# A mixture-of-experts kernel whose experts' inputs are fetched by indirect DMA and transposed, instead of gathered by matmuls

## The chip, the cores and the metric

The kernel runs on one core of one Trainium2 chip. Its time is device microseconds from launch to end. The kernel before took 3032.44 us (median of three runs, 3029.88 to 3035.55). TensorE is called PE, VectorE DVE, ScalarE ACT, GpSimd POOL and SyncE SP, as in the profile.

## The reference, cut to what matters

The program is a chain of four layers: two first ones and two equal blocks, each of a mixing phase and a mixture of experts. The change is in the mixture. It takes 512 tokens of 1024 numbers, chooses for each token two of 16 experts (from the group of four that holds the best score), and sums the two experts' outputs with their weights:

```python
def grouped_moe(x2d, w_router, router_bias, w_gate, w_up, w_down):
    ...                                   # scores, best group, two experts per token, weights
    buf_tok = jnp.full((P,), T, jnp.int32).at[dest].set(tok_flat[order])
    ...
    xb = x_pad[buf_tok].reshape(n_blocks, EXPERT_BLOCK, D)
    def expert_block(args):
        xblk, e = args
        h = jax.nn.silu(xblk @ w_gate[e]) * (xblk @ w_up[e])
        return h @ w_down[e]
    yb = lax.map(expert_block, (xb, blk_expert))
    y = yb.reshape(P, D) * buf_gate[:, None]
    return jax.ops.segment_sum(y, buf_tok, num_segments=T + 1)[:T]
```

All tensors are float32. The three weight matrices of one expert are 1024 x 512, 1024 x 512 and 512 x 1024, 6.3 MB together, so that the 16 experts of a layer read 100.7 MB.

## The kernel before, in words

Every float32 product is made of three matmuls of numbers that are split into a high and a low part (`mm3` and `tm`, lines L184 to L186): high by high, low by high, high by low. A weight chunk of 512 KB comes from memory on SP's queue (`wload`, L1602) into one of nine raw buffers (five named `mr`, four named `wr`); ACT casts it to the high part (`wsplit`, L1616), DVE subtracts to get the low part (L1617). A raw buffer is free for the next chunk when that subtraction has read it. Ten chunks are asked for before the experts begin.

Each expert owns 128 slots. Tokens beyond that go to overflow blocks, which a loop with a run-time count works through before the experts (`For_i` in `moe`). For an ordinary pair of experts `expert_slots` (L1650) compares each token's rank with the slot numbers, eight comparisons of 128 x 128, which give a 0/1 matrix `oh` for two experts. These run on DVE for experts 0 and 1 and on POOL for all others. `expert_in` multiplies the normed tokens, kept in SBUF as a high and a low part (`xs`, tiles named `x`), by that matrix: 64 matmuls of 128 x 256 at L1639, whose results are the pair's inputs, already transposed (`xg`, high part `xgh`, low part `xgl`). So the gather and the transposition are one product. `expert_up` multiplies by the gate and up weights, 48 matmuls, multiplies the two (`hs`, L1661 on DVE), and transposes `hs` by four matmuls at L1664; `expert_down` multiplies by the down weights, 24 matmuls, and writes the rows to a table `yd` in memory through ACT's queue. Experts are pipelined by one: expert e's up product is followed by the down product of expert e-1.

After expert 14's rows are written, eight indirect DMAs on POOL's queue (L1751) fetch, for each of four tiles of 128 tokens, the rows of its two experts out of `yd` into tiles `yg`; `add` (L1760, DVE) and `combine` (PE and DVE, L1768 to L1771) sum them with the token's own normed input. Expert 15's output does not go through `yd`; the matrix `oh` of its slots, transposed, spreads it over the tokens.

The order on each engine is made by a scheduler from its own estimates; `tc.issue_after(x)` holds instructions behind x. Buffers named `f4` (six of 128 x 1024) are shared by the matrices `oh`, the first gather of each token tile, and the raw weights of overflow blocks.

Of the kernel before, what the change touches and what calls it, by code (L numbers as in the profile page):

```python
# [18 lines left out]
P = 128  # L19
T = 512  # L20
# [28 lines left out]
class K:  # L49
# [1346 lines left out]
    def after_mix(self, l, xs, i0, gb, pl, sc, x1):  # L1396

        nc = self.nc
        tt = nc.vector.tensor_tensor
        st = self.ln_stats(xs[i0:i0 + 2])  # L1400
        u = self.small([2, 16], name="ru2")
        bc = lambda v: v[:, :, None].to_broadcast([P, 2, 16])
        bt = lambda v: v[:, None, :].to_broadcast([P, 2, 16])
        tt(u, bt(self.wsum[:, l, 0]), bc(st[:, 2]), op=OP.mult)
        tt(u, u, bt(self.wsum[:, l, 1]), op=OP.add)
        yield
        c = slice(i0, i0 + 2)
        tt(sc[:, c], pl[:, i0 * 16:(i0 + 2) * 16].rearrange("p (i e) -> p i e", i=2), bc(st[:, 1]), op=OP.mult)
        tt(sc[:, c], sc[:, c], u, op=OP.add)
        yield  # L1410
        late = i0 > 0
        for a in range(2):
            x = xs[i0 + a]
            t = self.x2()
            self.normal(x, st, a)
            for v in range(2):
                eng = AFFINE[late][a][v]
                with self.tc.issue_after(self.ranked.ins) if late else nullcontext():
                    getattr(nc, eng[0]).tensor_tensor(t[v], x[v], gb[0][v], op=OP.mult)  # L1419
                    getattr(nc, eng[1]).tensor_tensor(t[v], t[v], gb[1][v], op=OP.add)  # L1420
            h, lo = [self.wp.tile([P, D], F32R, name="x1", tag="xt", bufs=8) for _ in range(2)]
            x1[i0 + a] = h, lo
            for v in range(2):
                o = slice(v * 512, (v + 1) * 512)
                self.hi(h[:, o], t[v])
                with self.tc.issue_after(self.routed.ins) if late else nullcontext():
                    self.lo(lo[:, o], t[v], h[:, o])

    def moe_constants(self):
# [26 lines left out]
        for l in range(2):  # L1456
            for j, name in enumerate(("ln1_g_2", "ln1_b_2")):
# [7 lines left out]
                if j:  # L1465
                    nc.vector.tensor_tensor(s, s, rb, op=OP.add)
        self.yd = self.dp.tile([SLOTS, D], F32, name="yd")

    def clear_slots(self):

# [171 lines left out]
            xT += [(h[:, u * n:(u + 1) * n], lo[:, u * n:(u + 1) * n]) for u in range(2)]  # L1642
        return xT

    def expert_slots(self, rank, e, eng):

        oh = self.f4(F32R, "oh").rearrange("p (i a s) -> p i a s", i=4, a=2)
        for a in range(2):
            for i in range(4):
                eng.tensor_scalar(oh[:, i, a], self.iota, rank[:, i, e + a:e + a + 1], None, op0=OP.is_equal)  # L1650
        return oh.rearrange("p i a s -> p i (a s)")

    def expert_up(self, xT, wg, wu):

# [22 lines left out]
    def moe(self, l, xs, rt):  # L1677
# [10 lines left out]
        with tc.For_i(0, nov, 1) as b:  # L1688
# [9 lines left out]
            xT = self.expert_in(xs, oh.rearrange("p i a s -> p i (a s)"), 256)  # L1698
            hT = self.expert_up([[v[:, :P] for v in t] for t in xT], self.wrows(we[0], 8, True), self.wrows(we[1], 8, True))
            self.expert_down(hT, we[2], self.yd[bass.ds(row, P)], True)  # L1700
        oh = self.expert_slots(rank, 0, nc.vector)
        xT = self.expert_in(xs, oh, 256)
        hT = None
        f = []
        for e in range(16):
            if e % 2 == 0 and e < 14:
                oh = self.expert_slots(rank, e + 2, nc.gpsimd)
                nx = self.expert_in(xs, oh, 256)
            if e == 15:
                self.expert_down(hT, W[2][14], self.yd[14 * P:15 * P])  # L1710
            o = e % 2 * P
            h2 = self.expert_up([[v[:, o:o + P] for v in t] for t in xT],
                                *[self.wrows(W[j][e], 8, first=first.pop(0) if first else None) for j in range(2)])
            if e == 2:
                slot, wv, wl = self.weigh(oh1, oh2, sc, slotf)
            if e == 13:
                after = self.last_pe
            if e == 14:
                for i in range(4):
                    with tc.issue_after(after.ins):  # L1720
                        f.append(self.x2())
                        for h in range(2):
                            o = slice(h * 512, (h + 1) * 512)
                            nc.gpsimd.tensor_tensor(f[i][h], xs[i][0][:, o].bitcast(F32), xs[i][1][:, o].bitcast(F32), op=OP.add)
            if 0 < e < 15:
                self.expert_down(hT, W[2][e - 1], self.yd[(e - 1) * P:e * P])
            hT = h2
            if e % 2:
                xT = nx

        pt = self.pt()
        for i in range(4):
            nc.tensor.transpose(pt[:, i * P:(i + 1) * P], oh[:, i, P:].bitcast(F32), self.ident)
        ct = self.t2(F32R, "ct")
        nc.scalar.copy(ct, pt)
        pw = self.pt()
        for i in range(4):
            nc.tensor.matmul(pw[:, :1], oh[:, i, P:].bitcast(F32), wl[:, i:i + 1], start=i == 0, stop=i == 3)
        dg = self.t2(F32, "dg")
        for i in range(2):  # L1740
            for j in range(2):
# [29 lines left out]
                nc.vector.tensor_tensor(f[i][h], f[i][h], ps, op=OP.add)  # L1771

        y = []
        for c in range(2):
            py = self.pj()
            ws2 = list(self.wsplit(raws[c]))
            if c:
                for i in range(2):
                    for j in range(2):
                        add(i, j)  # L1780
            for k, wk in enumerate(ws2):
                self.mm3(py, hT[k], wk, k == 0, k == 3)
                if c == 1 and k == 1:
# [183 lines left out]
```

## Time and profile before

| | |
|---|---|
| median of three runs | 3032.44 us |
| profiled execution: its own time, span | 3038.98 us, 3037.2 us |
| busy PE, DVE, ACT, POOL | 2896.9, 1951.3, 1557.7, 271.0 us |
| DMA moved, mean rate | 453.48 MB, 149 GB/s |
| matmuls at L1639 | 1088, 136.2 us busy |
| granted TensorE clock, mean | 0.981 |

Busy shares are means over a span whose stages differ. Slice 22 of the 40 begins near 1595 us and holds the start of the first block's experts; the second block's experts fill slices 36 to 40. The DMA share of a window is the mean busy share of 16 DMA engines; a share near 1.00 reads as all of them busy, and the sum of packet times can come a little over it.

### The profile page before, as it was taken

The page shows a single profiled execution, that of the slowest core. Times are in us where ns is not written, and L with a number is a line of the kernel's source. Part 1 is how long each engine was busy: PE and PEld are TensorE (multiplying, and loading weights), DVE is VectorE, ACT ScalarE, POOL GpSimd, SP SyncE. Part 2 cuts the span into 40 slices and gives each one's busy share as a digit, 9 for nine tenths or more (in the row PEclk, how much of TensorE's full clock was granted, in tenths as well). Part 3 has the DMA queues.
Part 4 walks back from the last instruction along what each step waited for, and adds up shares of the span by engine and source line. Part 5 has one row for each costly group of instructions (what it writes and reads, how often), then busy time and mean ns, then how long its engine had stood idle before and what let it go on. Part 6 is the DMA issues. An engine that isn't in the chain of part 4 may idle for free. (4 is left out here: it accounts for less than half of the span.)

```text
span 3037.2 us, 44080 instructions
## 1 busy us (share of the span) xinstructions
PE 2896.9 (95%) x16635; PEld 2454.0 (81%) x16635; DVE 1951.3 (64%) x3817; ACT 1557.7 (51%) x2717; POOL 271.0 (9%) x282
## 2 busy tenths in 40 slices
PE   8999999999999999999989999879999999699996
PEld 6888878876669998878888888669987878588874
DVE  4454467576656776444477878978744345777788
ACT  4343377466655455223345777535542244476774
POOL 0000000000000000000027000440000000260023
PEclk9999999999999999999999999989999999899998
DMA  4242325431026222322365988931223335378996
GB/s 133 85 148 81 105 84 160 141 91 36 25 84 205 70 60 66 97 88 80 103 201 196 330 320 322 320 98 59 64 78 96 90 111 167 112 277 302 326 324 239
DMA packets 335599, 453.48 MB, mean 149 GB/s; under 512 B 24374, under 2 KB 208408, under 8 KB 335384
## 3 DMA queue, kind: packets, MB, share of 16 engines
q1 hardware_dynamic: 320856, 421.78, 42.1%
q10 hardware_dynamic: 12224, 20.46, 1.8%
q0 software_dynamic: 2304, 8.39, 0.8%
q8 instruction: 132, 2.16, 0.3%
q14 instruction: 83, 0.68, 0.1%
HBM read 421.69 MB, written 28.88 MB: 148 GB/s over the span
## 5 line engine op out<-in xcount | busy, mean ns | idle before, releaser
L164 DVE TENSOR_TENSOR wl<-wr,wh 128x1024 fp32r<-128x1024 f32 x348 | 422.9, 1217 | 441.1 <-ACT wh L163 436.9
L163 ACT CAST wh<-wr 128x1024 fp32r<-128x1024 f32 x352 | 363.1, 1033 | 579.9 <-PE pj L185 336.6
L184 PE MATMUL pj<-x,wh 128*128 128x512 f32 x1288 | 508.2, 395 | 0.6 <-ACT x L110 0.6
L185 PE MATMUL pj<-x,wh 128*128 128x512 f32 x1288 | 507.6, 394 | 0.0
L186 PE MATMUL pj<-x,wl 128*128 128x512 f32 x1288 | 506.3, 393 | 1.1 <-DVE wl L164 1.0
L186 PEld LDWEIGHTS pj<-x,wl 128*128 128x128 f32 x1288 | 241.9, 188 | 54.9 <-issue 4.7
L184 PEld LDWEIGHTS pj<-x,wh 128*128 128x128 f32 x1288 | 242.0, 188 | 52.6 <-issue 4.6
L185 PEld LDWEIGHTS pj<-x,wh 128*128 128x128 f32 x1288 | 242.0, 188 | 52.3 <-issue 5.6
L211 PE MATMUL pj<-wh,x 128*128 128x256 f32 x864 | 249.1, 288 | 3.8 <-DVE xb L277 3.1
L212 PE MATMUL pj<-wl,x 128*128 128x256 f32 x864 | 247.2, 286 | 0.0
L213 PE MATMUL pj<-wh,x 128*128 128x256 f32 x864 | 245.3, 284 | 0.0
L211 PE MATMUL pj<-wh,yh 128*128 128x256 f32 x640 | 181.6, 284 | 0.5 <-ACT wh L163 0.3
L212 PE MATMUL pj<-wl,yh 128*128 128x256 f32 x640 | 179.6, 281 | 1.5 <-DVE wl L164 1.5
L213 PE MATMUL pj<-wh,yl 128*128 128x256 f32 x640 | 179.1, 281 | 0.4 <-DVE yl L127 0.3
L211 PEld LDWEIGHTS pj<-wh,x 128*128 128x128 f32 x864 | 166.3, 193 | 5.2 <-DVE xb L277 3.5
L212 PEld LDWEIGHTS pj<-wl,x 128*128 128x128 f32 x864 | 166.6, 193 | 0.4
L213 PEld LDWEIGHTS pj<-wh,x 128*128 128x128 f32 x864 | 166.3, 193 | 0.3
L1639 PE MATMUL pt<-oh,x 128*128 128x256 f32 x1088 | 136.2, 287 | 18.4 <-DVE oh L1695 8.6
L1617 DVE TENSOR_TENSOR wl<-mr,wh 128x1024 fp32r<-128x1024 f32 x106 | 139.1, 1312 | 22.3 <-ACT wh L1616 22.2
L1639 PEld LDWEIGHTS pt<-oh,x 128*128 128x128 f32 x1088 | 135.3, 195 | 20.2 <-DVE oh L1695 8.7
L1617 DVE TENSOR_TENSOR ml<-mr,mh 128x1024 fp32r<-128x1024 f32 x108 | 135.9, 1258 | 21.5 <-ACT mh L1616 19.4
L1419 POOL TENSOR_TENSOR x<-x,bc 128x512 f32<-128x512 f32 x14 | 18.2, 1321 | 1255.7 <-ACT x L1328 1255.7
(503 smaller groups left out, 6607.0 us busy)
## 6 DMA issues: line engine op xcount, KB each, us to landing
wr<-in_w_in SPq DMA_DIRECT2D x124, 512.0 KB, 3.7
mr<-in_w_exp_gate SPq DMA_DIRECT2D x76, 512.0 KB, 6.6
mr<-in_w_exp_up SPq DMA_DIRECT2D x72, 512.0 KB, 5.5
mr<-in_w_exp_down SPq DMA_DIRECT2D x66, 512.0 KB, 5.9
wr<-in_w_exp_down SPq DMA_DIRECT2D x62, 512.0 KB, 6.3
wr<-in_hawk_w_in SPq DMA_DIRECT2D x60, 512.0 KB, 3.6
wr<-in_w_exp_up SPq DMA_DIRECT2D x56, 512.0 KB, 4.4
wr<-in_w_exp_gate SPq DMA_DIRECT2D x52, 512.0 KB, 6.9
```

Of the source, the lines that this page charges most:

```text
L163: self.nc.scalar.copy(wh[:, :kt, :c], raw[:, :kt, :c])
L164: eng.tensor_tensor(wl[:, :kt, :c], raw[:, :kt, :c], wh[:, :kt, :c].bitcast(F32), op=OP.subtract)
L184: mm(ps, a[0], b[0], start=first, stop=False)
L185: mm(ps, a[0], b[1], start=False, stop=False)
L186: mm(ps, a[1], b[0], start=False, stop=last)
L211: mm(d, tok(x[k][0]), w[k][0][:, :n], start=k == 0 and a == 0, stop=False, skip_group_check=True)
L212: mm(d, tok(x[k][0]), w[k][1][:, :n], start=False, stop=False, skip_group_check=True)
L213: mm(d, tok(x[k][1]), w[k][0][:, :n], start=False, stop=end, skip_group_check=True)
L1419: getattr(nc, eng[0]).tensor_tensor(t[v], x[v], gb[0][v], op=OP.mult)
L1617: self.nc.vector.tensor_tensor(wl, raw, wh.bitcast(F32), op=OP.subtract)
L1639: nc.tensor.matmul(pt[:, u * n:(u + 1) * n], xs[i][part][:, f], oh[:, i], start=i == 0 and part == 0, stop=i == 3 and part == 1)
```

## The change

The normed tokens are written to a table `x1d` in memory when they are made (`put`, eight stores of 256 KB per layer on SP's queue). `slot_tokens` works out on DVE, with eight small matmuls, which token sits in each slot of each expert (`idx`). `expert_fetch` then fetches the 128 rows of one expert by one indirect DMA on POOL's queue, 14 per layer, two experts ahead, and `expert_turn` transposes them by eight 128 x 128 matmuls and splits the result. Experts 0 and 1 and the overflow blocks keep the product with the 0/1 matrix; for expert 15 the matrix is still made, for the spread at the end. Seven of the eight pair products of a layer, 448 matmuls at L1639, and 52 of 56 comparisons on POOL are gone. The additions of token tiles 0 and 1 are held behind `mark`, the last split of expert 15's activations.

```diff
+            self.put(self.x1d[l], i0 + a, t)
...
+    def slot_tokens(self, ohs, rank):
...
+        for j, oh in enumerate(ohs):
+            tt(a, oh, rank, op=OP.mult)
+            nc.vector.tensor_reduce(r[:, j], a, axis=AX.X, op=OP.add)
+            for u in range(2):
+                tt(tk[:, j, :, u], oh, tok[:, u], op=OP.mult)
+            for i in range(4):
+                nc.vector.tensor_scalar(at[:, j, i], self.iota, r[:, j, i:i + 1], None, op0=OP.is_equal)
...
+                nc.tensor.matmul(ps[:, :32], at[:, j, i], tk[:, j, i].rearrange("p u e -> p (u e)"),
...
+    def expert_fetch(self, l, idx, e):
+        xg = self.f4(F32, "xg")
+        self.nc.gpsimd.indirect_dma_start(out=xg, out_offset=None, in_=self.x1d[l],
+                                          in_offset=bass.IndirectOffsetOnAxis(ap=idx[:, e:e + 1], axis=0))
...
+    def expert_turn(self, xg):
+        for h4 in range(2):
+            pt = self.pt()
+            for k in range(4):
+                f = (4 * h4 + k) * P
+                self.nc.tensor.transpose(pt[:, k * P:(k + 1) * P], xg[:, f:f + P], self.ident)
+            h, lo = self.split(pt, 1.0, "xg")
...
+        idx = self.slot_tokens((oh1, oh2), rank)
+        fetched = {e: self.expert_fetch(l, idx, e) for e in (2, 3)}
...
         for e in range(16):
-            if e % 2 == 0 and e < 14:
-                oh = self.expert_slots(rank, e + 2, nc.gpsimd)
-                nx = self.expert_in(xs, oh, 256)
+            if e == 12:
+                oh = self.expert_slots(rank, 15, 1, nc.gpsimd)
+            if 0 < e < 15:
+                xT.append(self.expert_turn(fetched.pop(e + 1)))
+                if e < 13:
+                    fetched[e + 3] = self.expert_fetch(l, idx, e + 3)
...
+        mark = self.split_end[0]
...
             if c:
-                for i in range(2):
-                    for j in range(2):
-                        add(i, j)
+                with tc.issue_after(mark.ins):
+                    for i in range(2):
+                        for j in range(2):
+                            add(i, j)
```

On PE, between one expert's down product and the next expert's gate product in the first block, the kernel before has this (`hh` and `hl` are the activations' parts, `pt` and `pj` PSUM tiles; the numbered `x` are the tokens' parts):

```order
L184 MATMUL pj<-mh,hh 128x512
L185 MATMUL pj<-ml,hh 128x512
L186 MATMUL pj<-mh,hl 128x512
L1639 MATMUL pt<-oh,x_14736 128x256
L1639 MATMUL pt<-oh,x_14737 128x256
L1639 MATMUL pt<-oh,x_14750 128x256
L1639 MATMUL pt<-oh,x_14751 128x256
L1639 MATMUL pt<-oh,x_14954 128x256
```

and the changed kernel this:

```order
L184 MATMUL pj<-mh,hh 128x512
L185 MATMUL pj<-ml,hh 128x512
L186 MATMUL pj<-mh,hl 128x512
L1701 MATMUL pt<-ident,xg 128x128 x8
L184 MATMUL pj<-wh,xgh 128x512
L185 MATMUL pj<-wl,xgh 128x512
L186 MATMUL pj<-wh,xgl 128x512
```

The block of 64 products has given way to eight transposes per expert, which wait for `xg` from memory.

On POOL, over all the experts of the first block, the comparisons before:

```order
L1650 TENSOR_SCALAR oh<-iota,rank 128x128 x56
L1724 TENSOR_TENSOR x<-x_14736,x_14737 128x512 x2
L1724 TENSOR_TENSOR x<-x_14750,x_14751 128x512 x2
L1724 TENSOR_TENSOR x<-x_14954,x_14955 128x512 x2
L1724 TENSOR_TENSOR x<-x_14968,x_14969 128x512 x2
L1751 DMA yg<-yd,rslot 128x1024 x7
L1743 TENSOR_SCALAR dg<-ident,rw 128x128 x4
L1751 DMA yg<-yd,rslot 128x1024
```

and after, where 14 fetches stand in their place:

```order
L1690 DMA xg<-x1d_1406,idx 128x1024 x13
L1652 TENSOR_SCALAR oh<-iota,rank 128x128 x4
L1690 DMA xg<-x1d_1406,idx 128x1024
L1780 TENSOR_TENSOR x<-x_14740,x_14741 128x512 x2
L1780 TENSOR_TENSOR x<-x_14756,x_14757 128x512 x2
L1780 TENSOR_TENSOR x<-x_14962,x_14963 128x512 x2
L1780 TENSOR_TENSOR x<-x_14978,x_14979 128x512 x2
L1805 DMA yg<-yd,rslot 128x1024 x7
L1797 TENSOR_SCALAR dg<-ident,rw 128x128 x4
L1805 DMA yg<-yd,rslot 128x1024
```

The gathers out of `yd` and the additions around them stay as they were, behind the fetches.

On DVE, at the end of the first block's experts, before:

```order
L1617 TENSOR_TENSOR ml<-mr,mh 128x1024
L1661 TENSOR_TENSOR hs<-hs,pj 128x512
L1617 TENSOR_TENSOR wl<-wr,wh 128x1024
L1617 TENSOR_TENSOR ml<-mr,mh 128x1024
L125 TENSOR_TENSOR hl<-pt,hh 128x512
L1745 COPY ws<-pt 128x1
L1760 SCALAR_TENSOR_TENSOR x<-yg,rw,x 128x512 x5
L127 SCALAR_TENSOR_TENSOR yll<-pj,ws,ylh 128x512
L1760 SCALAR_TENSOR_TENSOR x<-yg,rw,x 128x512 x3
L1771 TENSOR_TENSOR x<-x,pj 128x512 x2
```

and after (L1814 is `add`, L1714 the product `hs`, L1619 the subtraction of the weights):

```order
L1619 TENSOR_TENSOR wl<-mr,wh 128x1024
L1814 SCALAR_TENSOR_TENSOR x<-yg,rw,x 128x512
L1714 TENSOR_TENSOR hs<-hs,pj 128x512
L1619 TENSOR_TENSOR ml<-mr,mh 128x1024
L1619 TENSOR_TENSOR wl<-wr,wh 128x1024
L125 TENSOR_TENSOR hl<-pt,hh 128x512
L1799 COPY ws<-pt 128x1
L1619 TENSOR_TENSOR ml<-mr,mh 128x1024
L1814 SCALAR_TENSOR_TENSOR x<-yg,rw,x 128x512 x3
L127 SCALAR_TENSOR_TENSOR yll<-pj,ws,ylh 128x512
L1814 SCALAR_TENSOR_TENSOR x<-yg,rw,x 128x512 x5
L1825 TENSOR_TENSOR x<-x,pj 128x512 x2
```

The held additions now stand behind the split at L125, but one addition that is not held, of token tile 2 and so with the third gather on POOL's queue, stands ahead of expert 15's `hs`. The second block's rows are the same.

## Rows read from the trace of the kernel before

**Rows 1.** The page's 40 slices of the span: PE, granted clock and DMA in tenths.
```profile
PE   8999999999999999999989999879999999699996
PEclk9999999999999999999999999989999999899998
DMA  4242325431026222322365988931223335378996
```

**Rows 2.** By windows, one pair of experts: length, busy us (instructions) of PE, PEld, DVE, ACT, POOL; clock; DMA share; GB/s.
```profile
2829.48:2871.25 41.77, 41.77 (x219) 35.21 (x218) 33.60 (x33) 31.02 (x36) 0.00 (x0) 1.00 0.92 327
```

**Rows 3.** By windows, expert 0's first matmul to the last gather's issue, both layers.
```profile
1634.20:1967.60 333.40, 327.54 (x1629) 271.02 (x1628) 274.54 (x261) 240.57 (x278) 64.27 (x48) 0.99 0.89 317
2671.30:3004.40 333.10, 325.73 (x1617) 270.35 (x1615) 271.16 (x256) 240.37 (x278) 66.34 (x51) 0.99 0.89 316
```

**Rows 4.** By windows, four stretches in which the DMA engines are full.
```profile
1683.00:1711.00 28.00, 28.00 (x153) 23.85 (x152) 23.34 (x23) 21.54 (x26) 0.00 (x0) 1.00 1.02 368
1722.00:1752.00 30.00, 30.00 (x159) 25.31 (x158) 25.94 (x25) 23.07 (x27) 0.00 (x0) 1.00 1.02 364
1812.00:1842.00 30.00, 30.00 (x165) 25.70 (x164) 22.86 (x23) 21.44 (x27) 0.00 (x0) 1.00 0.95 345
2896.00:2921.00 25.00, 25.00 (x143) 21.67 (x142) 19.44 (x19) 17.88 (x22) 0.00 (x0) 1.00 1.01 369
```

**Rows 5.** By windows, the edges of layer 1's stretch.
```profile
2671.00:2675.00 4.00, 4.00 (x19) 3.25 (x19) 1.95 (x2) 2.59 (x3) 4.00 (x7) 1.00 0.00 0
2990.00:3004.40 14.40, 12.84 (x63) 9.72 (x61) 13.97 (x20) 6.72 (x9) 12.39 (x11) 1.00 0.85 287
```

**Rows 6.** By windows, line L1639 alone in layer 1's stretch.
```profile
2671.30:3004.40 333.10, 46.21 (x384) 46.06 (x384) 0.99 0.89 316
```

**Rows 7.** Timeline of PE: start, us, line, tiles, count [idle before <- releaser].
```profile
1617.62 16.72 PE L1639 MATMUL pt<-oh,x 128*128 128x256 f32 x128 [5.28 <-ACT mh L1616]
1634.18 0.39 PE L184 MATMUL pj<-wh,xgh 128*128 128x512 f32 x1
1634.41 0.39 PE L185 MATMUL pj<-wl,xgh 128*128 128x512 f32 x1
2653.89 17.34 PE L1639 MATMUL pt<-oh,x 128*128 128x256 f32 x128 [4.50 <-DVE oh L1650]
```

**Rows 8.** Timeline of PE, four transposes of hs and the next instruction.
```profile
2994.80 0.66 PE L1664 MATMUL pt<-ident,hs 128*128 128x128 f32 x4 [0.78 <-DVE hs L1661]
2995.30 0.60 PE L1733 MATMUL pt<-ident,oh 128*128 128x128 f32 x4
```

**Rows 9.** Timeline of PE, a matmul after an idle time.
```profile
2737.68 0.63 PE L186 MATMUL pj<-mh,xgl 128*128 128x512 f32 x1
```

**Rows 10.** The queue of POOL on the page, then its gathers by the tile yg.
```profile
q0 software_dynamic: 2304, 8.39, 0.8%
L1751 POOL DMA_INDIRECT yg<-yd,rslot x16: 933/1014/2107, 1949.2 to 3004.4; - x16
DMA to landing us min/median/max: 5.2/5.8/8.3
```

**Rows 11.** Waits of SP's queue, 2671 to 2986: us in total, times, longest.
```profile
SPq L1602 <- DVE ml L1617: 139.3, 87, 6.9
```

**Rows 12.** Timelines of DVE and POOL at layer 1's end.
```profile
2994.06 0.69 DVE L1661 TENSOR_TENSOR hs<-hs,pj 128x512 f32<-128x512 f32 x1 [0.25 <-PE pj L186]
2997.60 3.39 DVE L1760 SCALAR_TENSOR_TENSOR x<-yg,rw,x 128x512 f32<-128x512 f32 x5
2988.96 2.11 POOL L1751 DMA_INDIRECT yg<-yd,rslot  x1 [27.60 <-DMA mr<-in_w_exp_down]
2992.66 1.97 POOL L1751 DMA_INDIRECT yg<-yd,rslot  x1 [0.30 <-issue]
```

**Rows 13.** Timeline of DVE, small operations before the experts.
```profile
2652.73 1.72 DVE L1650 TENSOR_SCALAR oh<-iota,rank 128x128 fp32r<-128x128 f32 x8 [8.49 <-DMA yd<-yo]
```

**Rows 14.** Timeline of SP's queue, the first expert weights of layer 0.
```profile
1598.38 3.72 SPq L1602 DMA_DIRECT2D wr<-in_w_exp_up  x3
```

More of the change, by code (lines that the diff above doesn't have):

```diff
@@ L1467, in moe_constants @@
         self.yd = self.dp.tile([SLOTS, D], F32, name="yd")
+        self.x1d = [self.dp.tile([T, D], F32, name=f"x1d{l}") for l in range(2)]
     def clear_slots(self):
@@ L1643, in expert_in, with expert_slots @@
         return xT
-    def expert_slots(self, rank, e, eng):
-        oh = self.f4(F32R, "oh").rearrange("p (i a s) -> p i a s", i=4, a=2)
-        for a in range(2):
+    def expert_slots(self, rank, e, n, eng):
+        oh = self.f4(F32R, "oh")[:, :4 * n * P].rearrange("p (i a s) -> p i a s", i=4, a=n)
+        for a in range(n):
             for i in range(4):
@@ L1700, in moe @@
             self.expert_down(hT, we[2], self.yd[bass.ds(row, P)], True)
-        oh = self.expert_slots(rank, 0, nc.vector)
-        xT = self.expert_in(xs, oh, 256)
+        oh = self.expert_slots(rank, 0, 2, nc.vector)
+        xT = [[[v[:, a * P:(a + 1) * P] for v in t] for t in xT] for xT in [self.expert_in(xs, oh, 256)] for a in range(2)]
+        idx = self.slot_tokens((oh1, oh2), rank)
+        fetched = {e: self.expert_fetch(l, idx, e) for e in (2, 3)}
         hT = None
@@ L1705, in moe @@
         for e in range(16):
-            if e % 2 == 0 and e < 14:
-                oh = self.expert_slots(rank, e + 2, nc.gpsimd)
-                nx = self.expert_in(xs, oh, 256)
+            if e == 12:
[4 more added lines that the diff above has]
+                    fetched[e + 3] = self.expert_fetch(l, idx, e + 3)
             if e == 15:
                 self.expert_down(hT, W[2][14], self.yd[14 * P:15 * P])
-            o = e % 2 * P
-            h2 = self.expert_up([[v[:, o:o + P] for v in t] for t in xT],
-                                *[self.wrows(W[j][e], 8, first=first.pop(0) if first else None) for j in range(2)])
+            h2 = self.expert_up(xT[e], *[self.wrows(W[j][e], 8, first=first.pop(0) if first else None) for j in range(2)])
             if e == 2:
@@ L1727, in moe @@
             hT = h2
-            if e % 2:
-                xT = nx
         pt = self.pt()
         for i in range(4):
-            nc.tensor.transpose(pt[:, i * P:(i + 1) * P], oh[:, i, P:].bitcast(F32), self.ident)
+            nc.tensor.transpose(pt[:, i * P:(i + 1) * P], oh[:, i].bitcast(F32), self.ident)
         ct = self.t2(F32R, "ct")
@@ L1737, in moe @@
         for i in range(4):
-            nc.tensor.matmul(pw[:, :1], oh[:, i, P:].bitcast(F32), wl[:, i:i + 1], start=i == 0, stop=i == 3)
+            nc.tensor.matmul(pw[:, :1], oh[:, i].bitcast(F32), wl[:, i:i + 1], start=i == 0, stop=i == 3)
         dg = self.t2(F32, "dg")
@@ L1777, in moe @@
             if c:
-                for i in range(2):
-                    for j in range(2):
-                        add(i, j)
+                with tc.issue_after(mark.ins):
+                    for i in range(2):
+                        for j in range(2):
+                            add(i, j)
             for k, wk in enumerate(ws2):
```

22 lines of the change are left out of this document (added).

## The prediction

> **What bounds the kernel now.** I read the page's slices first. PE is busy nearly everywhere, and the DMA row reads 8 or 9 in four slices of the first block and 8, 9, 9, 6 at the very end, while it reads 1 to 6 elsewhere [rows 1]. Those are the experts of the two blocks, the stretches that the change edits. Next the windows. In a settled pair of experts PE is busy 41.77 of 41.77 us, DVE 33.60, ACT 31.02, POOL 0.00, and the DMA share is 0.92 [rows 2]. Over a whole layer, from expert 0's first matmul to the issue of the last gather, the stretch is 333.4 and 333.1 us long, PE is busy 327.54 and 325.73, and the DMA engines are busy 0.89 of it at 317 and 316 GB/s [rows 3]. So PE ends last, but the DMA engines are close behind it, with 11% to spare. That is the crux, since the change takes work from PE and gives work to DMA.
>
> How fast can DMA run? In four stretches of 25 to 30 us, 113 us together, the share is 1.02, 1.02, 0.95 and 1.01, mean 1.00, at 368, 364, 345 and 369 GB/s, mean 361 [rows 4]. What holds the loads back elsewhere is buffers: SP's queue waits 139.3 us, 87 times, for DVE's subtraction to free a raw buffer, never more than 6.9 us at once [rows 11]. A buffer comes free when PE, through ACT and DVE, asks for the next split weight, so a faster PE frees buffers earlier and pulls the loads forward, until the engines are full.
>
> **The change part by part.** I work per layer, with layer 1's stretch of 333.1 us.
>
> PE loses 46.21 us at L1639 inside the stretch [rows 6], and one block of 64 ahead of it: 128 matmuls take 16.72 and 17.34 us, so half of that is 8.4 and 8.7, I take 8.5 [rows 7]. It gains eight transposes per expert. Four take 0.50 us from their start to the next instruction's [rows 8], so eight take 1.0 and 14 experts 14. If PE alone set the pace the stretch would be 325.7 - 46.2 + 14 + 7.4 (its idle time now) = 300.9 us, 32.2 less.
>
> DMA gains 14 fetches. The same instruction on the same queue, the gather out of `yd`, has its price in the trace: 16 of them are 0.8% of 16 engines over 3037.2 us, or 24.3 us, so one is 1.52 us of all engines, and 14 are 21.3 us [rows 10]. The work in the stretch now is 333.1 x 0.89 = 296.5 us [rows 3]; with the fetches it is 317.8. Two edges cannot be filled: in the first 4.0 us the share is 0.00, since all buffers are full, and the last 14.4 us have 0.15 of idle, 2.2 us, because the gathers wait for rows [rows 5]. At a share of 1.00 the stretch is 317.8 + 6.2 = 324.0, 9.1 us less. By bytes: 316 GB/s over 333.1 us is 105.3 MB, the fetches add 14 x 8.39 / 16 = 7.3, and 112.6 MB at 361 GB/s are 312 us, 318 with the edges, 14.9 less. Both are longer than PE's 300.9, so after the change DMA sets the pace, and of PE's 32 us only 9.1 to 14.9 arrive. I take the middle, 12.0.
>
> The Trainium skill, "DMA: Bandwidth & Descriptors" (Specifications), gives about 358 GB/s as a core's share of memory bandwidth and 435 as the ceiling of the engines' own ports; its Measured section has 425 for one core alone. The full stretches here read 345 to 369, which agrees with the first figure. By 358 the 112.6 MB would take 315 us, 321 with the edges, close to my middle; by 425 they would take 265, and PE would set the pace, which is rival B below.
>
> The first block of 64 is gone ahead of expert 0 while the buffers are full, so its 8.5 us come back whole, whoever paces later. Bounds: 0, if the loads had to wait for it, and 8.7.
>
> The slot numbers cost DVE four small operations before expert 0; the others and their small matmuls lie between expert 0's products. Eight of the size took 1.72 us [rows 13], four cost 0.9. The first fetch can go after nine matmuls at 0.23 us (starts in rows 7) and these operations, some 4 us after expert 0 begins, is issued in 1.0 and lands 5.8 to 8.3 later [rows 10], 11 to 13 us in, against 11.1 us for expert 0's 48 products. PE may stall 0 to 2.5 us. While DMA sets the pace that costs nothing; if PE does, all of it. The later fetches are two experts ahead, some 40 us, and hide.
>
> The stores of `x1d` stand on SP's queue ahead of part of the weights. The first expert loads leave at 1598.38, 36 us before expert 0 [rows 14], and 2.1 MB take 5.8 us at 361 GB/s. I put 0, bounds 0 to 5.8.
>
> POOL's 52 comparisons go, where it is idle in the settled loop (0.00 above): 0. DVE's and ACT's work is nearly unchanged (the same splits, in other sizes) and lies below the new stretch: 271 and 240 us [rows 3].
>
> At the end one addition that needs the third gather now stands ahead of expert 15's `hs` on DVE. Before, `hs` ran at 2994.06, the third gather was issued at 2992.66 and with 5.8 us to land was there at about 2998.5, and the additions ran from 2997.60 [rows 12]. Behind `hs` are two subtractions, the split, and PE's last down product, all waiting. So `hs` would come 4.4 us late. Bounds: 0, if the gathers run earlier against `hs`, and 6.9, with the longest landing of 8.3. I take 4.4, the plain reading.
>
> **Sum.** Per layer -12.0 - 8.5 + 0.9 + 4.4 = -15.2 (from -12.3 to -18.1 by the two ways of counting DMA), for two layers -30.4. The profiled execution is 3038.98 us, the median 3032.44, 0.9978 of it; 3038.98 - 30.4 = 3008.6 profiled, 3002 as a median. With -24.6 and -36.2 it is 3008 and 2996.
>
> **The rivals.**
>
> B, PE still paces. The fetches ride in slack that the share does not show, or the engines run faster when asked. For it: PE is the one fully busy engine. Against it: a rate over 369 GB/s appears in none of the full stretches. Per layer -32.2 - 8.5 + 0.9 + 4.4 = -35.4, twice -70.8: 2968 profiled, 2962. Between A and B lies a DMA share that can reach 1.05: 317.8 / 1.05 + 6.2 = 308.9, per layer -27.4, which is 2977.
>
> C, no gain. The fetches of 4 KB rows, mixed with the weights, keep the share that can be held at about 0.96: 317.8 / 0.963 + 6.2 = 336.2, 3.1 more than now, and the 3.2 us of the other terms (8.5 - 0.9 - 4.4) go into it. For it: 0.95 stands among the full stretches. 3020 to 3040.
>
> D, slower: the mixture of weights, fetches and writes of `yd` holds no more than a share of 0.93, barely over the 0.92 of a settled pair. Then the stretch is 317.8 / 0.93 + 6.2 = 347.9, 14.8 more, less 3.2 is 11.6 per layer: 3062 profiled, 3055. Below 0.963 the change loses. Against it: 1.02 and 1.01 were held over 25 us and more.
>
> E, the clock. When PE waits for weights again and again, it runs slower: after an idle time at 2737 a matmul took 0.63 us [rows 9], where 0.39 is usual [rows 7], and the clock row dips in the slices where PE is less busy [rows 1]. One us at that speed loses 1 - 0.39 / 0.63 = 0.38. PE has 17 to 23 us of slack against the new DMA pace (318 or 324 less 300.9), so it decides from 45 to 60 us per layer at the slow speed; a third of the stretch, 111 us, would give 300.9 + 42 = 343, 10 over now, less 3.2, and 3046.
>
> **How the numbers follow.** A, DMA sets the pace: 0.60, with 2977 to 3008 as its own range. B 0.14. C 0.12, of which 0.04 faster, 0.06 same, 0.02 slower. D 0.08. E 0.06. About 0.2%, 6 us, is what can be told from no change here. Faster is 0.60 + 0.14 + 0.04 = 0.78, same 0.06, slower 0.02 + 0.08 + 0.06 = 0.16. The range takes in B and most of C: 2957 to 3035; it leaves out the far side of B, D and E.
>
> **What would show it.** L1639 should have 1088 - 896 = 192 matmuls in all, and the stretch from expert 0 to the last gather should be 318 to 324 us plus about 4, with a DMA share of 0.96 to 0.99 and PE busy for some 294 us (325.7 - 46.2 + 14), its idle time now released by the weights' subtraction. A fetch should land in 6 to 10 us and no transpose should wait for one after expert 2. The `hs` of expert 15 should start 4 us or so after its product is ready. Wrong would be: a DMA share still near 0.9 with PE full (B), a share that stays below 0.96 with PE idle (C, D), or matmuls of 0.6 us in the middle of the stretch (E). If the additions no longer wait, the end term falls away and the time is 9 us shorter.

## The result: 33 us faster, and what the profile after shows

The changed kernel took 2998.87 us (median of four runs, 2992.82 to 3004.20) against 3031.85 us before (also four runs); the ratio is 0.9889, 95% interval 0.9868 to 0.9911. The forecast was 3002. The profiled execution has a span of 3002.4 us, 34.8 less than before.

The page's slices and the row of POOL's queue, in answer to [rows 1] and [rows 10]:

```profile
PE   7999999999999999999998999869999999789995
PEclk9999999999999999999999999979999999899997
DMA  4242324431016322233265999832223334579995
...
q0 software_dynamic: 6336, 23.07, 2.0%
```

The same two stretches as in [rows 3] (expert 0's first matmul to the last gather's issue), and then two long windows in their middle. The columns are those of [rows 2].

```profile
1627.60:1937.25 309.65, 292.15 (x1325) 230.06 (x1323) 264.75 (x269) 234.83 (x280) 46.59 (x38) 0.99 1.01 367
2649.90:2959.45 309.55, 291.90 (x1326) 229.20 (x1326) 263.40 (x266) 235.00 (x280) 47.16 (x38) 0.99 1.00 365
1667.00:1777.00 110.00, 106.88 (x490) 86.66 (x491) 95.64 (x94) 87.97 (x106) 5.75 (x6) 0.98 1.04 388
2690.00:2860.00 170.00, 165.78 (x763) 132.29 (x763) 148.28 (x145) 136.05 (x164) 12.32 (x10) 1.00 1.04 382
```

The stretch fell from 333 us to 310, the DMA share rose from 0.89 to about 1.00, and in the middle the engines carry 382 to 388 GB/s at a share of 1.04, more than the full stretches of [rows 4] had (mean 361).

The issue of the last gather turned out a poor mark, since the additions that it waits behind have moved. A better one is PE's last matmul of expert 15's up product. From expert 0's first matmul to there, the kernel before:

```profile
1634.18:1953.42 319.24, 314.94 (x1573) 262.13 (x1572) 260.69 (x240) 236.98 (x273) 54.52 (x38) 0.99 0.90 319
2671.06:2993.64 322.58, 316.77 (x1574) 263.76 (x1572) 260.67 (x240) 236.92 (x273) 57.22 (x44) 0.99 0.89 316
```

and the changed kernel:

```profile
1627.60:1927.67 300.07, 288.82 (x1310) 227.11 (x1308) 260.44 (x264) 232.04 (x277) 38.40 (x29) 0.99 1.01 366
2649.83:2949.99 300.16, 288.06 (x1309) 225.74 (x1308) 258.92 (x261) 232.85 (x277) 39.09 (x29) 1.00 1.00 365
```

PE needs 288 to 289 us of work in place of 315 to 317, DVE and ACT nearly what they had, and PE, 99% and 98% busy before, now has 11 to 12 us idle. With this mark and, for the end of layer 0, the second L1319 on DVE behind it (1996.70 us before, 1979.01 after), the 34.8 us divide like this:

| part | before | after | difference |
|---|---|---|---|
| to expert 0's first matmul, layer 0 | 1634.18 | 1627.60 | -6.6 |
| experts, layer 0 | 319.2 | 300.1 | -19.2 |
| from the last up matmul to the second L1319, layer 0 | 43.3 | 51.3 | +8.1 |
| from there to expert 0 of layer 1 | 674.4 | 670.8 | -3.5 |
| experts, layer 1 | 322.6 | 300.2 | -22.4 |
| from the last up matmul to the end | 43.6 | 52.4 | +8.9 |

So the experts gained some 21 us per layer, more than forecast, and the end of each layer gave 8 to 9 back, also more than forecast. The end of layer 0 reaches a little past its mark. PE's first product of the next phase waits for `xb` there, before and after:

```profile
2004.87 0.58 PE L211 MATMUL pj<-wh,x 128*128 128x256 f32 x1 [3.10 <-DVE xb L277]
```

```profile
1989.98 0.58 PE L211 MATMUL pj<-wh,x 128*128 128x256 f32 x1 [6.16 <-DVE xb L277]
```

That matmul starts 8.2 us behind the mark before and 11.0 after, so 2.8 us of the end's loss stand in the table's fourth row.

PE's timeline shows the removed block of 64 in both layers (what is left takes 9.13 and 10.56 us, where [rows 7] had 16.72 and 17.34), eight transposes of one expert, and, at the end of layer 1, the last up matmul, the transposes of `hs` and a matmul behind them:

```profile
1618.62 9.13 PE L1641 MATMUL pt<-oh,x 128*128 128x256 f32 x64 [4.82 <-ACT wh L1618]
...
2639.43 10.56 PE L1641 MATMUL pt<-oh,x 128*128 128x256 f32 x64 [4.46 <-DVE oh L1652]
...
2664.15 1.04 PE L1701 MATMUL pt<-ident,xg 128*128 128x128 f32 x8
...
2949.99 0.39 PE L186 MATMUL pj<-mh,xgl 128*128 128x512 f32 x1
2955.93 1.12 PE L1717 MATMUL pt<-ident,hs 128*128 128x128 f32 x4 [5.54 <-DVE hs L1714]
...
2959.83 0.63 PE L185 MATMUL pj<-wl,hh 128*128 128x512 f32 x1
```

The transposes have no idle time ahead of them and so wait for no fetch. The end does wait: PE is idle for 5.54 us ahead of `hs`'s transposes, and what follows runs at 0.63 us a matmul, not 0.39. By windows the granted clock from those transposes on, then at the slow matmuls, and just after them:

```profile
2955.90:2959.20 3.30, 3.27 (x16) 3.28 (x17) 2.93 (x3) 2.02 (x3) 3.30 (x3) 0.50 0.88 348
2959.30:2962.80 3.50, 3.50 (x9) 2.74 (x10) 3.29 (x5) 0.00 (x0) 1.00 (x1) 0.50 0.41 110
2963.20:2965.20 2.00, 2.00 (x10) 1.46 (x8) 0.00 (x0) 0.69 (x1) 0.00 (x0) 1.00 0.04 14
```

That is 0.50, the lower of the two levels (1.2 GHz), for 7 us after the idle time (the transposes, the small products behind them and some nine matmuls of expert 15's down product), and then 1.00 (2.4 GHz). Before the change PE was idle for 0.78 us there [rows 8], and the clock read 1.00. DVE shows what PE waited for, and POOL's queue has the gather, the third:

```profile
2954.33 0.94 DVE L1814 SCALAR_TENSOR_TENSOR x<-yg,rw,x 128x512 f32<-128x512 f32 x1 [5.30 <-DMA yg<-yd,rslot]
2955.20 0.68 DVE L1714 TENSOR_TENSOR hs<-hs,pj 128x512 f32<-128x512 f32 x1
```

```profile
2949.02 0.94 POOL L1805 DMA_INDIRECT yg<-yd,rslot  x1 [0.30 <-DMA wr<-in_w_exp_down]
```

The addition L1814 waits 5.30 us for a gather issued at 2949.02, and `hs`, whose product was ready at 2950.4, stands behind it. In [rows 12] `hs` ran first and the additions later.

Of the chain that ended last, four steps. Among layer 1's experts the chain before had no weight load in its steps; now weights and the gather are on it:

```profile
2671.23 10.44 DMA mr<-in_w_exp_gate
...
2743.09 8.96 DMA wr<-in_w_exp_down
...
2941.03 7.79 DMA wr<-in_w_exp_down
2949.02 5.22 DMA yg<-yd,rslot
```

Six weight loads stand on it between 2660 and 2752, and then no DMA step until 2941: PE's matmuls, with subtractions and splits on DVE between them, make up that part. In layer 0 it is three loads up to 1730, and then none until 1908.

The tile `xg` (columns as in [rows 10]):

```profile
L1701 PE MATMUL pt<-ident,xg x224: 270/272/276, 1641.8 to 2914.0; 128*128 128x128 f32 x112
L1690 POOL DMA_INDIRECT xg<-x1d,idx x28: 937/951/1434, 1633.7 to 2816.9; - x28
...
DMA to landing us min/median/max: 5.6/7.8/10.9
```

### The profile page after: what moved, and what is told of

Its sections match the earlier page's. It is cut to its first block, busy times and chain, and to the rows that moved or that the text cites. A ratio compares the mean times of both kernels' runs of the same rounds, so it can differ in the third digit from the quotient of the medians.

```text
span 3002.4 us, 42694 instructions
## 1 busy us (share of the span) xinstructions
PE 2836.4 (94%) x15979; PEld 2373.6 (79%) x15979; DVE 1943.6 (65%) x3853; ACT 1547.4 (52%) x2717; POOL 197.2 (7%) x210
## 5 line engine op out<-in xcount | busy, mean ns | idle before, releaser
L1619 DVE TENSOR_TENSOR ml<-mr,mh 128x1024 fp32r<-128x1024 f32 x108 | 137.0, 1269 | 8.6 <-ACT mh L1618 8.4
L1619 DVE TENSOR_TENSOR wl<-mr,wh 128x1024 fp32r<-128x1024 f32 x106 | 131.8, 1243 | 16.5 <-ACT wh L1618 16.4
L212 PEld LDWEIGHTS pj<-wl,yh 128*128 128x128 f32 x640 | 121.7, 190 | 2.4 <-DVE wl L164 1.9
L211 PEld LDWEIGHTS pj<-wh,yh 128*128 128x128 f32 x640 | 121.9, 190 | 1.5 <-ACT yh L114 0.6
L1618 ACT CAST wh<-mr 128x1024 fp32r<-128x1024 f32 x106 | 111.2, 1049 | 22.5 <-DMA mr<-in_w_exp_gate 10.6
```

The costliest lines, as they stand in the source:

```text
L211: mm(d, tok(x[k][0]), w[k][0][:, :n], start=k == 0 and a == 0, stop=False, skip_group_check=True)
L212: mm(d, tok(x[k][0]), w[k][1][:, :n], start=False, stop=False, skip_group_check=True)
L1618: self.nc.scalar.copy(wh, raw)
L1619: self.nc.vector.tensor_tensor(wl, raw, wh.bitcast(F32), op=OP.subtract)
```

## The experiments

The theory to test was: in the experts the DMA engines now set the pace, PE no longer does, and the end is lost to a wait in DVE's order. The rival: PE, with the freeing of raw buffers by ACT and DVE, still paces, and the full engines are only its mirror. Times are compared as ratios to the kernel before on the same chip, which read 3034 to 3036 in these sets.

**The DMA half alone.** To the kernel before, one unread fetch for each of experts 0 to 13 was added, of 128 consecutive rows of a weight matrix:

```diff
...
+            if e < 14:
+                with tc.issue_after(self.last_pe.ins):
+                    xg = self.f4(F32, "xg")
+                    nc.gpsimd.indirect_dma_start(out=xg, out_offset=None, in_=I["w_exp_down_2"].rearrange("l e k c -> (l e k) c"),
+                                                 in_offset=bass.IndirectOffsetOnAxis(ap=lin[:, 0:1], axis=0))
```

> The kernel before, with its products at L1639 as they were, and 14 indirect fetches of 128 rows of 4 KB per layer added on POOL's queue, spread over the experts, which nobody reads (the rows come from a weight matrix). It adds the DMA half of the change without its PE half. Theory (before, the engines had 11% to spare, 36 us per layer, and PE set the pace): 21 us of work fit in, 0 to 4 us per layer, so 0 to 8 above the 3035 of these chips. Rival (every fetch delays a weight load that PE is waiting for): 10 to 20 us per layer, 3055 to 3075.

Measured: 3038.07 us against 3036.17, ratio 1.0001 (0.9992 to 1.0010). By windows, expert 0's first matmul to the last up matmul:

```profile
1631.71:1952.07 320.36, 315.61 (x1573) 262.21 (x1572) 260.81 (x240) 236.11 (x273) 76.49 (x58) 0.99 0.93 336
2669.84:2992.55 322.71, 316.88 (x1573) 263.33 (x1572) 260.11 (x240) 236.71 (x273) 79.59 (x63) 0.99 0.93 336
```

The share rose from 0.90 and 0.89 to 0.93, the rate by 17 and 20 GB/s, and the length stayed within 1.1 us. Before, the engines had room for 14 fetches of this size.

**Twice the fetches.** The changed kernel, each fetch done twice into the same tile:

```diff
-        self.nc.gpsimd.indirect_dma_start(out=xg, out_offset=None, in_=self.x1d[l],
...
+        for _ in range(2):
+            self.nc.gpsimd.indirect_dma_start(out=xg, out_offset=None, in_=self.x1d[l],
...
```

> The changed kernel with each of the 28 fetches done twice into the same tile: 14 x 1.52 = 21 us more DMA work per layer, nothing more on PE, DVE and ACT. Theory (the DMA engines are at their ceiling of about 1.04 in the middle of the stretch, and PE has no longer the last word): most of it arrives, 13 to 20 us per layer, 26 to 40 in all: 3025 to 3039. Rival (PE and the freeing of buffers set the pace, the engines could do more): under 8 us, 2999 to 3007.

Measured: 3029.44 us, ratio 0.9976 (0.9967 to 0.9985), 30 us above the changed kernel. By windows, the two layers' experts, and a long window in the middle of layer 1:

```profile
1623.55:1937.12 313.57, 292.56 (x1309) 229.02 (x1308) 261.65 (x264) 232.81 (x276) 56.76 (x43) 0.98 1.01 374
2658.43:2971.46 313.03, 292.61 (x1310) 228.62 (x1308) 260.69 (x261) 232.56 (x277) 54.79 (x42) 0.98 1.01 373
2720.00:2900.00 180.00, 174.34 (x801) 138.23 (x800) 155.36 (x152) 142.47 (x172) 20.62 (x16) 1.00 1.04 390
```

The experts grew by 13.5 and 12.9 us with nothing added on PE's side but waiting (PE is busy 4 us more and idle for 20). But half of that is no load of the engines: POOL issues a tile's second fetch only when its first has landed, and so the first eight transposes wait, in layer 1 with this row (5.44 us in layer 0):

```profile
2679.34 1.94 PE L1702 MATMUL pt<-ident,xg 128*128 128x128 f32 x8 [5.94 <-DMA xg<-x1d,idx]
```

Expert 1's `hs` is transposed 6.3 and 6.4 us later than in the changed kernel for that reason. What the load of 14 more fetches cost is the rest, some 7 us per layer. The two layers make 14, more than the rival's 8, and more than the 0 to 1 us a layer of the kernel before; but the forecast of 13 to 20 per layer was met only with the wait's help. The middle reads 1.04 and 390 GB/s, hardly more than in the changed kernel, and no run here holds a share above 1.05 for 100 us.

**One fetch in place of 14.** Experts 2 to 15 all transpose one tile, which leaves out the own inputs of 13 of them; the instructions on the other engines stay.

```diff
-        fetched = {e: self.expert_fetch(l, idx, e) for e in (2, 3)}
+        fetched = {2: self.expert_fetch(l, idx, 2)}
...
-                xT.append(self.expert_turn(fetched.pop(e + 1)))
-                if e < 13:
-                    fetched[e + 3] = self.expert_fetch(l, idx, e + 3)
+                xT.append(self.expert_turn(fetched[2]))
```

> The changed kernel with one fetch per layer in place of 14; experts 2 to 15 all transpose that one tile, so PE, DVE and ACT have the same work and DMA has 13 x 1.52 = 20 us less per layer. Theory (DMA sets the pace): the experts run at PE's pace, its 12 us of idle time in the stretch go, so 9 to 12 us per layer and 18 to 24 in all: 2975 to 2981. The stall at the end stays. Rival (PE and the freeing of buffers set the pace): within 4 us of 2998.87.

Measured: 2984.55 us, ratio 0.9838 (0.9821 to 0.9854), 14 us below the changed kernel, less than expected.

```profile
1623.08:1914.46 291.38, 286.10 (x1310) 226.24 (x1308) 260.33 (x264) 232.32 (x277) 23.63 (x16) 1.00 0.98 354
2636.58:2931.76 295.18, 287.78 (x1310) 227.49 (x1308) 259.02 (x261) 233.19 (x277) 24.75 (x16) 0.99 0.97 348
```

The experts shrank by 8.7 and 5.0 us, and PE is still idle for 5 to 7. The direction is the theory's, the size is not: from one fetch to 14 a fetch costs 0.5 us, from 14 to 28, without the wait above, also 0.5, and neither is the 1.46 (1.52 / 1.04) that a full queue would ask for everywhere. Where the cost falls can be read on PE's timeline. This is when `hs` of an expert is transposed in layer 1, in us from expert 0's first matmul:

| expert | 1 | 3 | 5 | 7 | 9 | 11 | 13 |
|---|---|---|---|---|---|---|---|
| one fetch | 25.8 | 66.6 | 101.5 | 137.5 | 174.2 | 211.4 | 251.5 |
| changed kernel | 27.9 | 70.7 | 106.4 | 142.5 | 179.2 | 216.4 | 256.4 |
| twice the fetches | 34.3 | 78.7 | 117.0 | 155.3 | 192.0 | 229.3 | 269.3 |

Up to expert 7 the three drift apart; from there on they keep step to 0.1 us, though fetches are still on their way. Layer 0 shows the same. So DMA sets the pace of the first half of the experts only, and in the second half it is PE, with the work on DVE that its chain passes through.

**Half of each row.** The fetches bring 512 numbers in place of a row's 1024, and the transposes read them twice. The index is left as it was, so they are halves of other tokens' rows: the tokens' own inputs are left out, bytes and instructions are what is compared.

```diff
-        self.nc.gpsimd.indirect_dma_start(out=xg, out_offset=None, in_=self.x1d[l],
+        self.nc.gpsimd.indirect_dma_start(out=xg[:, :512], out_offset=None, in_=self.x1d[l].rearrange("t (a c) -> (t a) c", a=2),
...
-                f = (4 * h4 + k) * P
+                f = k * P
```

> The changed kernel with fetches that bring 512 of the 1024 numbers of a row (the transposes read the same half twice), so 2 KB descriptors and half of the bytes of 28 fetches; the instructions on all engines stay. Theory (the DMA engines set the pace of the experts): 14 fetches of 1.5 us give back 10.6 us per layer at most; PE is idle for 12 us of the changed kernel's stretch in layer 1 (284.4 busy of 296.5 up to the first gather), which is the room. 6 to 10 us per layer, 12 to 20 in all: 2979 to 2987. Rival (PE and the freeing of raw buffers by ACT and DVE set the pace, and the full DMA engines are only its mirror): within 4 us of 2998.87. Third (it is descriptors and not bytes that count): also nothing.

Measured: 2992.00 us, ratio 0.9853 (0.9837 to 0.9870).

```profile
1623.10:1919.77 296.67, 288.17 (x1310) 227.30 (x1308) 260.24 (x264) 231.80 (x277) 40.33 (x29) 0.99 0.99 358
2643.12:2940.98 297.86, 288.57 (x1310) 227.24 (x1308) 258.90 (x261) 232.96 (x277) 39.65 (x29) 0.99 0.99 356
```

The experts shrank by 3.4 and 2.3 us, a third of what was expected, some 40% of the effect of taking 13 fetches away. It agrees with a price by bytes, but is too small to tell that from a price by rows.

**The transposes twice.**

```diff
-            for k in range(4):
+            for k in (0, 1, 2, 3, 0, 1, 2, 3):
```

> The changed kernel with each of the eight transposes of an expert done twice into the same place, 112 more transposes per layer, 14 us more work on PE by 0.125 us each. Theory (DMA sets the pace, PE has 12 us of idle time per layer): most of it is swallowed, 2 to 6 us per layer, 4 to 12 in all: 3003 to 3011. Rival (PE sets the pace): all of it arrives, 28 us, 3027.

Measured: 2998.38 us, ratio 0.9882 (0.9866 to 0.9899): nothing, if one reads the time alone.

```profile
1621.58:1926.09 304.51, 297.45 (x1421) 242.44 (x1420) 262.40 (x265) 235.47 (x277) 45.20 (x30) 0.99 1.00 362
2638.55:2947.89 309.34, 299.99 (x1422) 243.51 (x1420) 261.70 (x263) 235.69 (x277) 44.50 (x30) 0.98 0.99 356
```

By the windows the experts grew by 4.4 and 9.2 us. The time did not, because the scheduler placed the additions otherwise in this kernel: all behind `hs`, and from the last up matmul to the marks of the table 42.7 us pass in layer 0 and 44.1 in layer 1, where the changed kernel needs 51.3 and 52.4 (43.3 and 43.6 before). Two effects cancelled. So this run shows, without having been made for it, that the whole loss at the ends goes when no addition stands ahead of `hs` and none waits behind it; in layer 1 the first gather leaves 6.1 us ahead of `hs` here, 5.1 before the change. PE's added work (8.6 and 11.9 us by the busy columns) arrives by half or more; the theory had most of it swallowed.

**All additions held.** The additions of token tiles 2 and 3 go behind the same mark:

```diff
-        for i in range(2, 4):
-            add(i, 0)
+        with tc.issue_after(mark.ins):
+            for i in range(2, 4):
+                add(i, 0)
```

> The changed kernel with the additions of token tiles 2 and 3 held behind the same mark as those of tiles 0 and 1, so that expert 15's hs no longer stands behind an addition that needs the third gather. Theory (the stall is a wait in the order on DVE, paid in full): in the changed kernel, from the start of expert 15's last up product to the end of the span, 52.4 us pass in layer 1 where 43.6 passed before, and 51.3 against 43.3 to the same small operation in layer 0. Both come back: PE's idle time of 5.5 and 6.3 us ahead of hs's transposes goes to under 1 us, the 9 to 12 matmuls at 0.63 us behind it go back to 0.39, and the time is 14 to 17 us below the changed kernel's 2998.87, about 2983. Rival (the gathers are the end of the stretch anyway, and the wait only moves to a later instruction): 0 to 6 us, 2993 to 2999.

Measured: 2990.40 us, ratio 0.9852 (0.9836 to 0.9869). Later, on one chip with the changed kernel:

> The changed kernel again, for a comparison on one chip: 2996 to 3002.

> The kernel with all additions held behind the mark again, on the same chip as the changed kernel. If what it won before was the wait and not the chip: 7 to 10 us below the changed kernel.

Measured: the changed kernel 2997.29, ratio 0.9871 (0.9855 to 0.9886); all additions held 2992.03, ratio 0.9858 (0.9843 to 0.9873). So 5.3 us on the same chip, where the intervals overlap, and 8.5 between the first sets: less than the 14 to 17 of the first forecast, and less than the second's 7 to 10. The wait ahead of `hs` did go (`hs` starts 0.4 us after the last up matmul in both layers), but DVE at the end of layer 1 has a new one:

```profile
2940.21 0.69 DVE L1714 TENSOR_TENSOR hs<-hs,pj 128x512 f32<-128x512 f32 x1 [1.39 <-PE pj L186]
...
2945.83 1.41 DVE L1814 SCALAR_TENSOR_TENSOR x<-yg,rw,x 128x512 f32<-128x512 f32 x2
2949.93 1.48 DVE L1814 SCALAR_TENSOR_TENSOR x<-yg,rw,x 128x512 f32<-128x512 f32 x2 [2.70 <-DMA yg<-yd,rslot]
2951.34 0.74 DVE L127 SCALAR_TENSOR_TENSOR yll<-pj,ws,ylh 128x512 fp32r<-128x512 f32 x1
```

Two additions further the queue waits 2.70 us for a gather, and `yll`, which PE needs and waits 2.27 us for, stands behind that. From `hs` to the end 49.2 us pass (46.7 in the later execution), 43.1 before. Part of the forecast gain had turned into a later wait.

**Held further back.** The mark is the first `yll` in place of the split; the additions of token tiles 2 and 3 are held behind it too, as above:

```diff
             if c:
+                mark = self.split_end[0]
                 with tc.issue_after(mark.ins):
...
```

> As the kernel that holds all additions behind the last split of expert 15's activations (2990.4 us), but held further back, behind the first yll, so that no addition stands on DVE ahead of what expert 15's down product needs. In that kernel four additions stood ahead of yll, waited 2.7 us for a gather, and PE waited 2.27 us for yll in layer 1; from hs to the end 49.2 us passed, where before the change 43.1 did. Theory (the end is lost to waits for gathers in DVE's order): these waits go, hs to the end is 44 to 46 us, and the time is 3 to 5 us per layer under 2990.4, so 2980 to 2984. Rival (the gathers are late against hs now, and the additions are on the path wherever they stand): 2988 to 2993.

Measured: 2992.95 us, ratio 0.9853 (0.9839 to 0.9866), no better. From `hs` to the end 49.6 us.

```profile
2941.60 0.69 DVE L1714 TENSOR_TENSOR hs<-hs,pj 128x512 f32<-128x512 f32 x1 [1.39 <-issue]
...
2949.56 0.75 DVE L127 SCALAR_TENSOR_TENSOR yll<-pj,ws,ylh 128x512 fp32r<-128x512 f32 x1 [2.26 <-ACT ylh L1843]
2950.22 5.38 DVE L1814 SCALAR_TENSOR_TENSOR x<-yg,rw,x 128x512 f32<-128x512 f32 x8
...
2956.72 0.75 DVE L127 SCALAR_TENSOR_TENSOR yll<-pj,ws,ylh 128x512 fp32r<-128x512 f32 x1
```

No addition waits here, and still nothing is won: eight of them, 5.38 us, now stand between the first and the second `yll`, while DVE idles 2.26 us ahead of the first. The theory of the single wait fell. That the additions fit behind `hs` only if the gathers have landed by then is argued from these rows; the doubled transposes above and the last kernel below agree with it, and no run was made to show it alone.

**Without the mark.**

```diff
-                with tc.issue_after(mark.ins):
-                    for i in range(2):
-                        for j in range(2):
-                            add(i, j)
+                for i in range(2):
+                    for j in range(2):
+                        add(i, j)
```

> The changed kernel without the mark, so that the additions stand where the scheduler puts them: two of them ahead of expert 15's hs instead of one. Theory (what counts is the latest gather that an addition ahead of hs needs): the third gather is needed already in the changed kernel, so the mark is worth nothing or the wait grows by the gap between two gathers, 1.3 us: 2998 to 3003. Rival (the mark is what keeps the end short): 8 us or more above 2998.87.

Measured: 2995.78 us, ratio 0.9865 (0.9850 to 0.9880), the same as the changed kernel within the interval.

```profile
2949.97 0.75 DVE L1814 SCALAR_TENSOR_TENSOR x<-yg,rw,x 128x512 f32<-128x512 f32 x1 [5.74 <-DMA yg<-yd,rslot]
...
2954.44 0.69 DVE L1714 TENSOR_TENSOR hs<-hs,pj 128x512 f32<-128x512 f32 x1 [0.79 <-PE pj L186]
```

An addition waits 5.74 us here too, a little earlier, ahead of weight subtractions, so the wait shows up inside the experts (307.4 and 306.0 us to the last up matmul). The mark alone, as the change sets it, is worth nothing that these runs can tell.

**Gathers earlier, less DMA at the end.** All additions held, and experts 14 and 15 by the 64 products again:

```diff
             if e == 12:
-                oh = self.expert_slots(rank, 15, 1, nc.gpsimd)
-            if 0 < e < 15:
+                oh = self.expert_slots(rank, 14, 2, nc.gpsimd)
+            if e == 13:
+                nx = self.expert_in(xs, oh, 256)
+                xT += [[[v[:, a * P:(a + 1) * P] for v in t] for t in nx] for a in range(2)]
+            if 0 < e < 13:
                 xT.append(self.expert_turn(fetched.pop(e + 1)))
-                if e < 13:
+                if e < 11:
...
```

> The kernel with all additions held (2990.4), in which experts 14 and 15 get their inputs from the 64 products with the 0/1 matrix again, which expert 15 needs anyway; 12 fetches per layer stay. Theory (DMA sets the pace, PE has some 12 us of idle time per layer, and the last gathers come late because the engines are full): 2 x 1.5 = 3 us less DMA work, 7.7 - 2.0 = 5.7 us more PE work, which fits into the idle time; the gathers run 1 us earlier against hs, and hs to the end is 44 to 46 us in place of 49.2 in layer 1. 3 to 6 us per layer, 2979 to 2985. Rival (near the end PE has no room left, and its 5.7 us arrive): 3 us per layer slower, 2996.

Measured: 2985.26 us (2981.60 to 2991.56), ratio 0.9845 (0.9831 to 0.9858), on the chip on which the changed kernel took 2997.29. By window, layer 1's experts from expert 0's first matmul to the last up matmul, then POOL's first gather and DVE's `hs` and additions:

```profile
2631.75:2934.03 302.28, 291.92 (x1358) 232.71 (x1356) 260.87 (x263) 233.30 (x277) 45.37 (x33) 1.00 0.99 362
```

```profile
2925.89 1.86 POOL L1808 DMA_INDIRECT yg<-yd,rslot  x1 [30.72 <-DMA yd<-yo]
```

```profile
2935.11 0.67 DVE L1714 TENSOR_TENSOR hs<-hs,pj 128x512 f32<-128x512 f32 x1
...
2938.45 3.97 DVE L1817 SCALAR_TENSOR_TENSOR x<-yg,rw,x 128x512 f32<-128x512 f32 x5
2943.39 0.75 DVE L127 SCALAR_TENSOR_TENSOR yll<-pj,ws,ylh 128x512 fp32r<-128x512 f32 x1 [0.97 <-ACT ylh L1845]
```

The first gather leaves 9.2 us ahead of `hs` (5.1 before the change, 3.2 in the kernel with all additions held), five additions run right behind the split, and `yll` waits only for ACT. From `hs` to the end 44.8 us pass (2979.9 less 2935.11). The experts themselves did not get shorter (302.3 us; 300.2 in the changed kernel), so in layer 1 the gain lies at the end: 45.9 us from the last up matmul on, where the changed kernel needs 52.4. By its median this is the fastest of the kernels that leave nothing out; its interval overlaps that of the kernel with the additions held, so of the two it is the likelier, not the proven better one. Whether the end gains by the earlier gathers or by the smaller DMA load was not taken apart.

## Why the prediction came out right, point by point

**Right.** PE no longer sets the pace alone: fetches that are free in the kernel before cost time in the changed one. The bytes and shares of the stretch: 316 GB/s and 0.89 became 365 and 1.00. The fetch's price of 1.52 us: 28 of them and 16 gathers are 2.0% of 16 engines' span, 961 us / 44 / 16 = 1.4 us each. PE's work: 294 us forecast, 291.9 measured over the same stretch. No transpose waited for a fetch, though a fetch took 7.8 us to land, not 5.8. The wait of `hs` at the end was seen from the order alone: 4.4 us forecast, 5.5 and 4.8 more delay measured. The hidden terms (stores of `x1d`, POOL's comparisons) are singled out by no row of the table. Of the part between the layers, with a block of 64 gone (-6.8) and -3.5 in all, 2.8 of the missing 3.3 us are the wait for `xb` at its start. The start of layer 0 differs by 9 us between two executions of the changed kernel (1627.60 and 1618.43), so its -6.6 is no test of the 8.5.

**Half right, the pace.** "DMA sets the pace" was meant for the whole stretch. The chain and the table of experts show it for the first half alone. PE had 26.1 and 28.7 us less work among the experts, and 19.2 and 22.4 of that arrived, about three quarters; the forecast was 12.0 of 32.2. The truth lies between A and B, near the case of a share of 1.05 that the prediction names there. The prediction also read the loads' waits short: the 139.3 us of [rows 11] are those for `ml`; for `wl` the same view has 92.1 us more, 50 times, at most 13.0.

**Mis-sized, the DMA term.** The prediction took "the middle, 12.0" from a ceiling of share 1.00 and 361 GB/s, and expected a stretch of 318 to 324 us plus about 4. Measured: 309.6 us, and by the table 19.2 and 22.4 in place of 12.0. The four full stretches of the kernel before were read as the engines' ceiling, but PE was at 100% in each of them [rows 4], so they show what PE asked for. With less work on PE the middle holds 1.04 and 382 to 390 GB/s, also with twice the fetches. With 1.04 the prediction's own sum gives 317.8 / 1.04 + 6.2 = 311.8, close to 309.6, but in part by luck: over the whole stretch the share is about 1.00, and by bytes 113 MB at 382 to 388 GB/s are 291 to 296 us, 297 to 302 with the edges, about PE's 300.9.

The Trainium skill, "DMA: Bandwidth & Descriptors" (Specifications), has about 358 GB/s for a core's share; its Measured section has 425 for a core that streams alone. The runs show 382 to 390 over windows of 100 us and more, so the share is no limit for one core here, and the higher figure was not reached by this mixture of weight chunks, fetched rows and writes.

**Mis-sized, the end.** The prediction charged 4.4 us for "the third gather"; the two ends cost 8.1 and 8.9. The wait itself is 5.5 (layer 0) and 4.8 (layer 1) of that. In layer 1 the gather left no later than before, 1.4 us ahead of the end of `hs`'s product (2949.02 and 2950.38; 2992.66 and 2994.03 before), and landed in 5.22; what the 4.4 left out is the addition's own 0.94 us. The rest lies behind `hs`, and the prediction put it at nothing: it is the clock of 0.50 after the idle time. From `hs`'s transposes to the first down matmul 3.33 us pass in both layers, 1.75 before; the slow ones of the down product start 0.43 us apart, not 0.23, which adds 1.5 us in layer 1 and 2.0 in layer 0. That is 3.1 to 3.6 us, and with the wait it accounts for the two ends to within 1 us. Rival E had named this cost, for the middle of the stretch, and by durations (1 - 0.39 / 0.63 = 0.38); by the starts one us at that clock loses 0.46.

The errors have opposite signs. Over both layers the experts gained 17.6 us more than forecast, the ends lost 8.2 more, and the start blocks with what surrounds them gained 5.1 less (10.1 in place of 15.2). The 30.4 us forecast came out as 34.8 in the profiled executions; that 3002 is so near to 2998.87 is in good part cancellation. Rival B's PE pace (2962) was not reached; even with one fetch the kernel took 2984.55, with the wait at the end still in it.

## What to carry to other kernels

A resource that reads "full" while another engine is at 100% has shown demand, not its ceiling; take the ceiling as open upward and keep a second price for it. When work moves from the bounding engine to one with little room, price the marginal unit on both sides: 14 fetches cost 0 to 1 us before the move and some 7 after it. Ask of an added load whether it also adds a wait: here that was half of the 13 us. And look at the end of a stage by itself: here an instruction that waited for a DMA and stood ahead of the critical product cost its wait (5 us) and the slow matmuls behind it (3 us), and holding it back won less than that, since later waits came in its place.

## What was not expected of the hardware

The DMA share stays at 1.04 for 110 to 180 us at 382 to 390 GB/s, so a share of 1.00 in this view is not the top. An indirect fetch is issued by POOL in 0.95 us (median) beside DVE's subtractions and lands in 5.6 to 10.9 us when the engines are full, 5.2 to 8.3 in [rows 10]. One fetch of 0.52 MB cost 0.5 us of time on average, all of it in the first half of the experts and nothing in the second. An idle time of 5.5 us on PE cost another 3 us behind it at a granted clock of 0.50.
